# An encoder trunk whose first norm and first gate projection are interleaved two slices at a time

## The chip, the core and the metric

The kernel runs on one core of one Trainium2 chip. The metric is device time in microseconds (us); three runs of the kernel before gave 1000.81, 1001.91 and 1004.33, with a median of 1001.91.

## What is computed

Two layers on 256 tokens of 1024 values in float32. Each layer is a feed-forward block, a mixer (gated linear attention in the first layer, differential attention in the second) and another feed-forward block, each with an RMS norm ahead and a residual sum behind. Cut to the part that matters here, the first feed-forward block:

```python
def rms_norm(x, g):
    xf = x.astype(jnp.float32)
    y = xf * lax.rsqrt(jnp.mean(xf * xf, axis=-1, keepdims=True) + EPS)
    return (y * g.astype(jnp.float32)).astype(x.dtype)

def swiglu_ffn(h, w_gu, w_down):
    gate, up = jnp.split(h @ w_gu, 2, axis=-1)
    return (jax.nn.silu(gate) * up) @ w_down

x = x + 0.5 * swiglu_ffn(rms_norm(x, norm_g[i, 0]), ffn_w_gu[i, 0], ffn_w_down[i, 0])
```

The 1024 values of a token are eight slices of 128. The gate and the up projection have 2816 columns each, taken in groups of 256.

## The kernel before

Everything is kept transposed: the features on the 128 partitions, the tokens along the row. To get float32 accuracy from the faster float32r matmul, each operand is split into a high and a low part. ScalarE (ACT) writes the high part, rounded; VectorE (DVE) subtracts it from the whole and writes the low part. One slice of a projection is then a matmul over 512 columns with the high part of the weights (L181) and one over 256 columns with their low part (L182), in `mm3`.

**Weights.** `weight_plan` lists all weights as pieces of 1024 x 256 in order of use: weights 0 is the first gate group, weights 1 the first up group, weights 2 the second gate group, and so on. `prefetch` (L111) loads them on SyncE's queue (SP) into three staging buffers. A load waits until the low part of the weights three places earlier has been made, which frees its buffer. `next_weights` (L165) is called where a projection begins: it prefetches, has `split_weights` (L142) issue the splits of weights up to three ahead, and hands out the weights wanted.

**What sets the order.** The program is recorded in the order of the Python calls. A scheduler then puts each engine's instructions into one order; an engine runs its own strictly in that order. `tc.issue_after(i)` keeps an operation behind `i` on its engine. `split_weights` issues every split behind the operations in `state["behind"]`. `rsqrt` (L208), which computes the inverse root of the row statistics with twelve tiny DVE operations, ends so:

```python
            last = nc.vector.scalar_tensor_tensor(out=y, in0=t, scalar=1.5, in1=y, op0=ALU.add, op1=ALU.mult)
        state["behind"] += (last,)
```

so whatever is split by a later call stands behind it on DVE.

**The start.** `first_norm` (L397) loads x in three pieces on SP, then prefetches. The norm's weights (`rows`) come by GpSimd's queue (L230). TensorE (PE) runs eight idle matmuls, transposes `rows` (L406), whose copy `par` scales x, and then makes 16 transposes of 128 x 128 that turn x around (L413). Neighbouring slices of x lie in different PSUM banks, "so that two engines can follow each other". Per two slices, ACT and DVE split x twice (L276, L277) and then a quarter of weights 0 (L422). After the last quarter DVE copies x out of PSUM (L426), with the split of weights 1 (L432) between the copies, and the squares of x are taken and summed into `acc` (L285, L288, L289).

In `ffn` (L441) the first call of `next_weights` hands out weights 0 for the first gate group. Behind it come `norm.stats()` (two matmuls of `acc` into `ps_ms`, L294, then `rsqrt`), the join of the two halves of the gate (L205, L206), and the up projection:

```python
                pg = project(next_weights(), norm.x2, f"ps_g{c}", together=first and c == 0)
                if c == 0:
                    norm.stats()
                    if not first:
                        release(*state["behind"])
                gate = fp.tile([P, 2, T], F32, tag="gate", name="gate")
                join(pg, gate)
                pu = project(next_weights(), norm.x2, f"ps_u{c}")
                if c == 0:
                    norm.spread()
```

`norm.spread()` turns the result `r` around on PE (`ps_r`, L302).

Of the kernel before, what the change touches and what calls it, by code (L numbers as in the profile page):

```python
# [37 lines left out]
# the differential mixer: h half a projection; for pair of heads p: bp statistics, np normalized q and k,  # L38
# sph scores and softmax of head h, fp the transposed probabilities, ap their products with v, op normalized; hold keeps weights
# from being split  # L40
# [3 lines left out]
# the gated linear attention: h half a projection; z the gate's logits, y its log decay, pi prefix sums of pair of  # L44
# heads i, ri its scores before decay, d l t the next level's decays, scores and place among the scores,
# ai products with v, gi output gate, oi normalized; hold keeps weights from being split, x lets them go
# [8 lines left out]
def weight_plan(w):  # L55
    """The weights in the order of use: [rows, columns] pieces of at most 1024 x 256, slices of rows, columns, copies."""
# [17 lines left out]
    # four times side by side, to have the ranks on four groups of partitions  # L74
# [16 lines left out]
def trunk(ctx: ExitStack, tc: tile.TileContext, ins, out):  # L91
# [31 lines left out]
    def parts():  # L123
        """The parts of the next weights to split."""
# [26 lines left out]
    def issue(ops, after):  # L151
        """Each operation behind those of `after` that run on its engine."""
        with ExitStack() as order:
            for i in after:
                order.enter_context(tc.issue_after(i.ins))
            for op in ops:
                op()  # L157

    def release(*after):
        """The parts held back, behind `after`."""  # L160
        issue(held, after)
        held.clear()
        state["hold"] = None
# [8 lines left out]
    def mm1(ps, w, ms, act, k, first, last):  # L172
        """ps += wh.xh + wh.xl + wl.xh for one 128-deep slice."""
# [4 lines left out]
    def mm3(ps, w, ms, act, k, first, last, wk=None):  # L178
        """ps[:, 0:256] += wh.xh + wl.xh, ps[:, 256:512] += wh.xl for one 128-deep slice."""
# [4 lines left out]
    def project(w, act, name, together=False):  # L184
        banks = [psA.tile([P, 512], F32, tag="A", name=f"{name}_{b}") for b in range(2)]
        order = [(b, k) for b in range(2) for k in range(KD)]
        for b, k in sorted(order, key=lambda bk: bk[1]) if together else order:
            mm3(banks[b], w, slice(b * P, (b + 1) * P), act, k, k == 0, k == KD - 1)
        return banks
# [11 lines left out]
    def join(banks, out_t):  # L201
        """out = both halves of three-pass products."""
# [5 lines left out]
    def rsqrt(v, shape, name):  # L208
        """v ** -0.5 for v > 0."""
# [20 lines left out]
    nc.gpsimd.dma_start(rows, ins["norm_g"].rearrange("l s (k p) -> (l s k) p", p=P))  # L230
    nc.vector.memset(warm, 0.0)
    # the tensor engine runs at half its clock until it has been busy for a while
# [18 lines left out]
    def load_gate(w2):  # L251
        """The second gate weights as rows of high, low, high, low parts, zero against the other direction's ranks."""
# [54 lines left out]
    def down(act, nk, coef, norm):  # L307
        """x += coef * act @ w, and the next norm's blocks as they come."""
# [26 lines left out]
    def out_proj(act, norm, parts, late):  # L335
        """x += act @ w; the two first column groups wait for `late` with their last slices."""
# [28 lines left out]
    def by_token(xt):  # L365
        """x with the tokens on the partitions."""
# [10 lines left out]
    def down_out(act, nk, coef, xt):  # L377
        """out = x + coef * act @ w, with the tokens on the partitions."""
# [18 lines left out]
    def first_norm():  # L397
        n = Norm(0)
        with ExitStack() as xctx:
            xp = xctx.enter_context(tc.tile_pool(name="xin", bufs=1))  # L400
            x_tm = xp.tile([P, 2, D], F32, name="x_tm")
            for cs in (slice(0, CW), slice(CW, D // 2), slice(D // 2, D)):
                nc.sync.dma_start(x_tm[:, :, cs], ins["x"][0].rearrange("(t p) c -> p t c", p=P)[:, :, cs])
            prefetch(0)
# [3 lines left out]
            # neighbouring blocks lie in different banks, so that two engines can follow each other  # L408
            tiles = [psA.tile([P, 2, T], F32, tag="A", name=f"ps_x{i}") for i in range(KD // 2)]
            xt = [tiles[k // 4 * 2 + k % 2][:, k // 2 % 2, :] for k in range(KD)]  # L410
            for k in range(KD):
                for t in range(2):
                    nc.tensor.transpose(out=xt[k][:, t * P : (t + 1) * P], in_=x_tm[:, t, k * P : (k + 1) * P], identity=ident)  # L413
            last = ()
            for kp, ops in enumerate(parts()):
# [5 lines left out]
                with tc.issue_after(last[0].ins), tc.issue_after(last[1].ins):  # L421
                    last = [op() for op in ops]  # L422

            def keep(kp):
                k = kp // 2 * 4 + kp % 2
                return nc.vector.tensor_copy(x[:, k : k + 3 : 2, :], tiles[kp])  # L426
# [12 lines left out]
        return n  # L439

    def ffn(norm, nxt, first=False, beside=None):  # L441
        with ExitStack() as fctx:
            fp = fctx.enter_context(tc.tile_pool(name="ffn", bufs=2))
            a2 = fp.tile([P, NFB, 2, T], FR, tag="a2", name="a2", bufs=1)
            for c in range(FF // CW):
                if first and c == 3:
                    load_params()
                    relative_bias()
# [4 lines left out]
                pg = project(next_weights(), norm.x2, f"ps_g{c}", together=first and c == 0)  # L453
# [28 lines left out]
    def gla(norm, nxt, w2):  # L482
        QK = KD // 2
        with ExitStack() as gctx:
# [7 lines left out]
            with tc.tile_pool(name="glb", bufs=2) as lp:  # L492
                # gate path: low rank -> log decay -> prefix sums per tile of 128 tokens
# [6 lines left out]
                # both directions' ranks, twice the high parts, twice the low ones  # L500
# [8 lines left out]
                def project_half(kind, c, n):  # L509
                    """Half a column group: of q and k half the columns, of v and g half the tokens."""  # L510
# [459 lines left out]
```

## Time and profile before

| | us |
|---|---|
| median of three runs | 1001.91 |
| fastest and slowest run | 1000.81, 1004.33 |
| span of the profiled execution, first to last instruction | 1000.1 |
| PE busy in it | 994.5 |
| DVE busy | 748.0 |
| ACT busy | 567.7 |
| GpSimd (POOL) busy | 2.0 |

The profiled execution's own device time is not listed beside its span; the fastest run is 0.7 us above the span and the median 1.8 us. Times in the rows are microseconds from the start of the span, means of one instruction are in ns. PE is the matmul, PEld the load of the stationary operand, which overlaps it; a lower-case q behind an engine is its queue, where it issues transfers and waits. A PE duration is the time until its result is out, so two neighbours overlap; the step from one start to the next, or the chain's pieces, tell what a matmul costs.

### The profile page before, as it was taken

To read this page: it belongs to the slowest core of one execution; us is meant where nothing else is said; L and a number is where in the kernel's file an instruction comes from. 1 tells how busy PE (TensorE), PEld (TensorE's weight loads), DVE (VectorE), ACT (ScalarE), POOL (GpSimd) and SP (SyncE) were. 2 spreads that over 40 slices of the span, in tenths; PEclk is the share of its full clock that TensorE was granted. 3 is DMA by queue.
4 is the path that set the end of the run, shared out by engine and by line. 5 is a ranking of instruction groups with operands and counts; after the bars stand their busy time and mean duration, and the time that the engine had idled before them with its cause. 6 is when DMAs were issued, how large, how long until landed. Compare 5 with 4: busy or idle time off the path is not lost.

```text
span 1000.1 us, 16172 instructions
## 1 busy us (share of the span) xinstructions
PE 994.5 (99%) x6524; PEld 906.6 (91%) x6524; DVE 748.0 (75%) x1284; ACT 567.7 (57%) x962; POOL 2.0 (0%) x10
## 2 busy tenths in 40 slices
PE   9999999999999999999999999999999999999998
PEld 8888888999999888888888888889999998888998
DVE  6998756499877987774679787656989699767640
ACT  7666535397756755643456555435576577555430
POOL 0000000000000000000000000000000000000000
PEclk9999999999999999999999999999999999999999
DMA  9676544574322775545557555375655268555440
GB/s 295 221 263 209 190 158 135 194 226 154 127 85 85 256 248 178 190 159 187 167 176 248 195 184 178 128 240 171 194 149 169 65 200 274 178 171 193 158 132 22
DMA packets 176968, 178.95 MB, mean 179 GB/s; under 512 B 4419, under 2 KB 176222, under 8 KB 176894
## 3 DMA queue, kind: packets, MB, share of 16 engines
q1 hardware_dynamic: 176606, 177.68, 54.3%
q8 instruction: 51, 0.84, 0.3%
q10 hardware_dynamic: 256, 0.21, 0.1%
q14 instruction: 23, 0.19, 0.1%
q0 software_dynamic: 32, 0.02, 0.0%
HBM read 176.84 MB, written 1.06 MB: 178 GB/s over the span
## 4 chain that ended last, share of the span: by engine, by line
PE 98%; DVE 1%; DMA 0%; ACT 0%; issue 0%; ACTq 0%; POOLq 0%
PE ps_g L181 16%; PE ps_u L181 16%; PE ps_d L181 12%; PE ps_g L182 8%; PE ps_u L182 8%; PE ps_d L182 6%; PE ps_d L388 2%; PE ps_d L389 2%; PE ps_d L390 2%; PE ps_s L567 2%; PE ps_dqk L196 2%; PE ps_dqk L198 2%; PE ps_dqk L197 2%; PE ps_w L174 1%; PE ps_w L176 1%; PE ps_w L175 1%
## 5 line engine op out<-in xcount | busy, mean ns | idle before, releaser
L157 DVE TENSOR_TENSOR w<-stage,w 128x1024 fp32r<-128x1024 f32 x334 | 385.4, 1191 | 32.2 <-ACT w L157 31.9
L157 ACT ACTIVATE w<-stage 128x1024 fp32r<-128x1024 f32 x334 | 327.3, 1030 | 45.4 <-PE ps_d L390 17.0
L181 PE MATMUL ps_g<-x,w 128*128 128x512 f32 x704 | 249.3, 397 | 0.0
L181 PE MATMUL ps_u<-x,w 128*128 128x512 f32 x704 | 248.7, 395 | 0.0
L182 PE MATMUL ps_u<-x,w 128*128 128x256 f32 x704 | 197.5, 281 | 0.0
L182 PE MATMUL ps_g<-x,w 128*128 128x256 f32 x704 | 197.1, 281 | 0.0
L181 PE MATMUL ps_d<-a,w 128*128 128x512 f32 x528 | 183.2, 390 | 0.0
L181 PEld LDWEIGHTS ps_g<-x,w 128*128 128x128 f32 x704 | 132.0, 188 | 31.0 <-issue 0.9
L181 PEld LDWEIGHTS ps_u<-x,w 128*128 128x128 f32 x704 | 132.0, 188 | 30.7
L182 PE MATMUL ps_d<-a,w 128*128 128x256 f32 x528 | 149.0, 282 | 0.0
L182 PEld LDWEIGHTS ps_g<-x,w 128*128 128x128 f32 x704 | 133.4, 189 | 0.5
L182 PEld LDWEIGHTS ps_u<-x,w 128*128 128x128 f32 x704 | 133.1, 189 | 0.1
L181 PEld LDWEIGHTS ps_d<-a,w 128*128 128x128 f32 x528 | 99.1, 188 | 20.7
L182 PEld LDWEIGHTS ps_d<-a,w 128*128 128x128 f32 x528 | 99.9, 189 | 0.0
L276 ACT ACTIVATE x<-x,par 128x256 fp32r<-128x256 f32 x40 | 20.0, 507 | 117.5 <-DVE x L325 117.5
L205 ACT COPY half<-ps_u 128x256 f32<-128x256 f32 x88 | 32.7, 371 | 87.2 <-PE ps_u L182 85.4
L205 ACT COPY half<-ps_g 128x256 f32<-128x256 f32 x88 | 32.3, 370 | 83.5 <-PE ps_g L182 81.4
L206 DVE TENSOR_TENSOR up<-ps_u,half 128x256 f32<-128x256 f32 x88 | 36.9, 422 | 38.7 <-ACT half L205 38.6
L206 DVE TENSOR_TENSOR gate<-ps_g,half 128x256 f32<-128x256 f32 x88 | 36.8, 422 | 36.9 <-ACT half L205 36.9
L325 DVE SCALAR_TENSOR_TENSOR x<-ps_d,x 128x256 f32<-128x256 f32 x48 | 20.3, 424 | 57.9 <-PE ps_d L182 56.7
L388 PE MATMUL ps_d<-w,a 128*128 128x256 f32 x176 | 49.5, 281 | 0.0
L389 PE MATMUL ps_d<-w,a 128*128 128x256 f32 x176 | 49.5, 281 | 0.0
(232 smaller groups left out, 1560.6 us busy)
## 6 DMA issues: line engine op xcount, KB each, us to landing
stage<-in_ffn_w_gu_dram SPq DMA_DIRECT2D x86, 1024.0 KB, 5.1
stage<-in_ffn_w_down_dram SPq DMA_DIRECT2D x32, 1024.0 KB, 4.8
stage<-in_ffn_w_down_dram SPq DMA_DIRECT2D x16, 768.0 KB, 4.1
stage<-in_gla_w_in_dram SPq DMA_DIRECT2D x12, 1024.0 KB, 5.6
stage<-in_diff_w_in_dram SPq DMA_DIRECT2D x12, 1024.0 KB, 5.5
stage<-in_gla_w_out_dram SPq DMA_DIRECT2D x4, 1024.0 KB
stage<-in_diff_w_out_dram SPq DMA_DIRECT2D x4, 1024.0 KB, 4.9
stage<-in_ffn_w_gu_dram SPq DMA_DIRECT2D x8, 256.0 KB, 5.7
```

What stands on the lines that cost most here:

```text
L157: op()
L181: mm(ps, lhsT=w[:, wk, 0, ms], rhs=act[:, k, :, :], start=first, stop=False)
L182: mm(ps[:, 0:T], lhsT=w[:, wk, 1, ms], rhs=act[:, k, 0, :], start=False, stop=last)
L196: mm(ps[:, t, :], lhsT=act[:, k, 0, ts_], rhs=w[:, k, 0, :], start=k == 0, stop=False)
L197: mm(ps[:, t, :], lhsT=act[:, k, 0, ts_], rhs=w[:, k, 1, :], start=False, stop=False)
L198: mm(ps[:, t, :], lhsT=act[:, k, 1, ts_], rhs=w[:, k, 0, :], start=False, stop=k == KD - 1)
L205: nc.scalar.copy(h[:, b, :], ps[:, T:512])
L206: nc.vector.tensor_tensor(out=out_t[:, b, :], in0=ps[:, 0:T], in1=h[:, b, :], op=ALU.add)
L325: nc.vector.scalar_tensor_tensor(out=x[:, d, :], in0=ps[:, h * T : (h + 1) * T], scalar=coef, in1=x[:, d, :], op0=ALU.mult, op1=ALU.add,)
L388: mm(ps, lhsT=act[:, k0 + k, 0, ts_], rhs=w[:, k, 0, :], start=first, stop=False)
L389: mm(ps, lhsT=act[:, k0 + k, 0, ts_], rhs=w[:, k, 1, :], start=False, stop=False)
L390: mm(ps, lhsT=act[:, k0 + k, 1, ts_], rhs=w[:, k, 0, :], start=False, stop=last)
```

## The change

x is loaded in four pieces instead of three. The four quarters of weights 0 are loaded between them, two on ACT's queue and two on SP. The norm's weights come by ACT's queue instead of GpSimd's. The table and one-hot matrix of the relative-position bias, which had been loaded on ACT's queue at the start, move behind later work. `first_norm` becomes `first_group`: it brings two slices at a time (transposes, splits of x, split of the quarter) and puts the first gate group's matmuls of two slices behind the next two slices' transposes. Two neighbouring slices now share a PSUM bank. The first gate group no longer goes through `project` and `next_weights`, so in `ffn` the first call of `next_weights` is that of the first up group.

```diff
-    nc.gpsimd.dma_start(rows, ins["norm_g"].rearrange("l s (k p) -> (l s k) p", p=P))
+    nc.scalar.dma_start(rows, ins["norm_g"].rearrange("l s (k p) -> (l s k) p", p=P))
...
-    def first_norm():
+    def first_group():
...
-            for cs in (slice(0, CW), slice(CW, D // 2), slice(D // 2, D)):
+            src, nk, width, _ = plan[0]
+            t0 = staged[0] = stage.tile([P, KD, CW], F32, tag="stage", name="stage0")
+            state["dma"] = 1
+            for kp in range(KD // 2):
+                cs, ks = slice(kp * CW, (kp + 1) * CW), slice(2 * kp, 2 * kp + 2)
                 nc.sync.dma_start(x_tm[:, :, cs], ins["x"][0].rearrange("(t p) c -> p t c", p=P)[:, :, cs])
+                q = nc.scalar if kp < 2 else nc.sync
+                q.dma_start(t0[:, ks, :], src.rearrange("(k p) n -> p k n", p=P)[:, ks])
             prefetch(0)
...
-            # neighbouring blocks lie in different banks, so that two engines can follow each other
             tiles = [psA.tile([P, 2, T], F32, tag="A", name=f"ps_x{i}") for i in range(KD // 2)]
-            xt = [tiles[k // 4 * 2 + k % 2][:, k // 2 % 2, :] for k in range(KD)]
-            for k in range(KD):
-                for t in range(2):
-                    nc.tensor.transpose(out=xt[k][:, t * P : (t + 1) * P], in_=x_tm[:, t, k * P : (k + 1) * P], identity=ident)
+            xt = [tiles[k // 2][:, k % 2, :] for k in range(KD)]
+            split_parts = list(parts())
+            banks = [psA.tile([P, 512], F32, tag="A", name=f"ps_g0_{b}") for b in range(2)]
+            w0 = split.pop(0)
+            state["use"] = 1
             last = ()
-            for kp, ops in enumerate(parts()):
+
+            def bring(kp):
+                nonlocal last
+                for k in (2 * kp, 2 * kp + 1):
+                    for t in range(2):
+                        nc.tensor.transpose(out=xt[k][:, t * P : (t + 1) * P], in_=x_tm[:, t, k * P : (k + 1) * P], identity=ident)
                 for k in (2 * kp, 2 * kp + 1):
                     with ExitStack() as order:
                         for i in last:
                             order.enter_context(tc.issue_after(i.ins))
                         last = n.split(k, xt[k])
                 with tc.issue_after(last[0].ins), tc.issue_after(last[1].ins):
-                    last = [op() for op in ops]
+                    last = [op() for op in split_parts[kp]]
+
+            bring(0)
+            for kp in range(KD // 2):
+                if kp + 1 < KD // 2:
+                    bring(kp + 1)
+                for k in (2 * kp, 2 * kp + 1):
+                    for b in range(2):
+                        mm3(banks[b], w0, slice(b * P, (b + 1) * P), n.x2, k, k == 0, k == KD - 1)
...
                 if first and c == 3:
                     load_params()
-                    relative_bias()
+                    with tc.issue_after(state["behind"][0].ins):
+                        relative_bias()
...
-                pg = project(next_weights(), norm.x2, f"ps_g{c}", together=first and c == 0)
+                pg = first if first and c == 0 else project(next_weights(), norm.x2, f"ps_g{c}")
```

How the change moves instructions shows at three places. First PE, between the first up group and the second gate group. Before, PE goes on with the second gate group (`ps_g_0_354`, `ps_g_1_355`, weights `w_220`), and the statistics `ps_ms` stand behind the first matmul of the second up group (`ps_u_0_401`, weights `w_225`), 33 rows on:

```order
L182 MATMUL ps_u_1_296<-x_0_101,w_178 128x256
L181 MATMUL ps_g_0_354<-x_0_101,w_220 128x512
L182 MATMUL ps_g_0_354<-x_0_101,w_220 128x256
L181 MATMUL ps_g_0_354<-x_0_101,w_220 128x512
...
L182 MATMUL ps_g_1_355<-x_0_101,w_220 128x256
L181 MATMUL ps_u_0_401<-x_0_101,w_225 128x512
L294 MATMUL ps_ms_264<-cst,acc_102 128x1 x2
L182 MATMUL ps_u_0_401<-x_0_101,w_225 128x256
```

In the change, at the same place (the second gate group is now `ps_g_0_355` and `ps_g_1_356` with `w_281`, the second up group `ps_u_0_402` and `ps_u_1_403` with `w_286`, the third gate group `ps_g_0_456` and `ps_g_1_457` with `w_291`):

```order
L182 MATMUL ps_u_1_297<-x_0_101,w_213 128x256
L181 MATMUL ps_g_0_355<-x_0_101,w_281 128x512
L181 MATMUL ps_g_1_356<-x_0_101,w_281 128x512
L181 MATMUL ps_u_0_402<-x_0_101,w_286 128x512
L181 MATMUL ps_u_1_403<-x_0_101,w_286 128x512
L294 MATMUL ps_ms_255<-cst,acc_102 128x1 x2
L181 MATMUL ps_g_0_456<-x_0_101,w_291 128x512
L181 MATMUL ps_g_1_457<-x_0_101,w_291 128x512
L302 MATMUL ps_r_330<-cst,r_y 128x128 x2
L182 MATMUL ps_g_0_355<-x_0_101,w_281 128x256
L181 MATMUL ps_g_0_355<-x_0_101,w_281 128x512
```

The statistics, `ps_r` and the first matmuls of three groups now stand ahead of the second gate group's first L182, which reads the low part of weights 2.

Second DVE, from the sum of squares on. Before, the low parts of weights 2 and 3 (`w_220`, `w_225`) stand among the sums of squares, ahead of the statistics (`var`):

```order
L289 TENSOR_TENSOR acc_102<-acc_102,sq 128x256
L157 TENSOR_TENSOR w_220<-stage_120,w_220 128x4x256
L289 TENSOR_TENSOR acc_102<-acc_102,sq 128x256
L157 TENSOR_TENSOR w_220<-stage_120,w_220 128x4x256
L289 TENSOR_TENSOR acc_102<-acc_102,sq 128x256
L157 TENSOR_TENSOR w_225<-stage_122,w_225 128x4x256
...
L206 TENSOR_TENSOR up<-ps_u_0_295,half 128x256
L296 TENSOR_SCALAR var_267<-ps_ms_264 128x2
```

In the change (`w_281`, `w_286`, `w_291` are weights 2, 3 and 4):

```order
L206 TENSOR_TENSOR up<-ps_u_1_297,half 128x256
L289 TENSOR_TENSOR acc_102<-acc_102,sq 128x256
L296 TENSOR_SCALAR var_258<-ps_ms_255 128x2
L212 TENSOR_SCALAR r_t<-var_258 128x2
...
L216 TENSOR_TENSOR r_t<-r_t,var_258 128x2
L217 SCALAR_TENSOR_TENSOR r_y<-r_t,r_y 128x2
L157 TENSOR_TENSOR w_281<-stage_121,w_281 128x4x256 x2
L157 TENSOR_TENSOR w_286<-stage_123,w_286 128x4x256 x2
L157 TENSOR_TENSOR w_291<-stage_125,w_291 128x4x256 x2
```

All six pieces now stand behind the last operation of `rsqrt`.

Third ACT, over the same stretch. Before, four squares and two copies stand around the splits of weights 2 and 3:

```order
L288 ACTIVATE sq<-x 128x256 x2
L205 COPY half<-ps_g_1_231 128x256
L157 ACTIVATE w_220<-stage_120 128x4x256 x2
L205 COPY half<-ps_u_0_295 128x256
L288 ACTIVATE sq<-x 128x256
L157 ACTIVATE w_225<-stage_122 128x4x256 x2
L288 ACTIVATE sq<-x 128x256
```

In the change:

```order
L157 ACTIVATE w_281<-stage_121 128x4x256 x2
L205 COPY half<-ps_u_0_296 128x256
L157 ACTIVATE w_286<-stage_123 128x4x256
L288 ACTIVATE sq<-x 128x256 x2
L157 ACTIVATE w_286<-stage_123 128x4x256
L288 ACTIVATE sq<-x 128x256 x2
L205 COPY half<-ps_u_1_297 128x256
L288 ACTIVATE sq<-x 128x256
L157 ACTIVATE w_291<-stage_125 128x4x256 x2
```

Five of the eight squares now stand behind the first piece of weights 3, and the last of them behind the copy of the first up group's second half.

## Rows read from the trace of the kernel before

**Rows 1.** The page: busy time of the engines, and the last chain's shares.

```profile
PE 994.5 (99%) x6524; PEld 906.6 (91%) x6524; DVE 748.0 (75%) x1284; ACT 567.7 (57%) x962; POOL 2.0 (0%) x10
...
PE 98%; DVE 1%; DMA 0%; ACT 0%; issue 0%; ACTq 0%; POOLq 0%
```

**Rows 2.** PE's waits over the whole span: us in total, times, longest.

```profile
PE ps_idle L235 <- DVE warm L231: 0.9, 1, 0.9
PE ps_doT L891 <- DVE do L883: 0.7, 1, 0.7
PE ps_rows L406 <- DMA rows<-in_norm_g_dram: 0.7, 1, 0.7
```

**Rows 3.** The chain that ended last, from 4 to 16 us: start, us, what.

```profile
1.23 4.10 DMA rows<-in_norm_g_dram
...
5.37 0.34 PE ps_rows L406
5.71 3.60 PE ps_x L413 x16
9.31 0.85 PE ps_g L181 x2
10.16 0.36 PE ps_g L182 x2
10.52 0.23 PE ps_g L181
10.75 0.12 PE ps_g L182
```

**Rows 4.** DMA issues of the first 60 us: queue, count, KB each, median us to landing.

```profile
stage<-in_ffn_w_gu_dram SPq DMA_DIRECT2D x12, 1024.0 KB, 5.3
...
rows<-in_norm_g_dram POOLq DMA_DIRECT2D x1, 24.0 KB, 4.1
tab<-in_rel_bias_table_dram ACTq DMA_DIRECT2D x1, 1.0 KB, 3.9
```

**Rows 5.** ACT by time, 5 to 9 us, and its first issue of `tab`.

```profile
1.21 0.50 ACTq L725 DMA_DIRECT2D tab<-in_rel_bias_table_dram  x1
...
7.28 0.84 ACT L276 ACTIVATE x<-ps_x,par 128x256 fp32r<-128x256 f32 x2 [1.33 <-PE ps_x L413]
8.02 0.62 ACT L422 ACTIVATE w<-stage 128x512 fp32r<-128x512 f32 x1
```

**Rows 6.** DVE by time, 5 to 16 us.

```profile
7.78 0.88 DVE L277 SCALAR_TENSOR_TENSOR x<-ps_x,par,x 128x256 fp32r<-128x256 f32 x2 [6.92 <-ACT x L276]
8.67 0.69 DVE L422 TENSOR_TENSOR w<-stage,w 128x512 fp32r<-128x512 f32 x1
9.28 0.87 DVE L277 SCALAR_TENSOR_TENSOR x<-ps_x,par,x 128x256 fp32r<-128x256 f32 x2
...
12.83 0.69 DVE L422 TENSOR_TENSOR w<-stage,w 128x512 fp32r<-128x512 f32 x1
```

**Rows 7.** SP's queue by time: the issue that waits for `oh`, then the load of weights 3.

```profile
6.37 0.37 SPq L119 DMA_DIRECT2D stage<-in_ffn_w_gu_dram  x1
...
13.54 0.37 SPq L119 DMA_DIRECT2D stage<-in_ffn_w_gu_dram  x1
```

**Rows 8.** ACT by time, 14 to 20 us.

```profile
13.50 1.14 ACT L432 ACTIVATE w<-stage 128x512 fp32r<-128x512 f32 x2
...
15.39 0.73 ACT L288 ACTIVATE sq<-x 128x256 f32<-128x256 f32 x2
16.02 0.36 ACT L205 COPY half<-ps_g 128x256 f32<-128x256 f32 x1
16.27 2.01 ACT L157 ACTIVATE w<-stage 128x1024 fp32r<-128x1024 f32 x2
```

**Rows 9.** DVE by time, 24 to 50 us.

```profile
25.44 0.43 DVE L289 TENSOR_TENSOR acc<-acc,sq 128x256 f32<-128x256 f32 x1
...
27.34 0.16 DVE L296 TENSOR_SCALAR var<-ps_ms 128x2 f32<-128x2 f32 x1 [1.14 <-PE ps_ms L294]
...
28.55 0.15 DVE L215 SCALAR_TENSOR_TENSOR r_t<-r_y 128x2 f32<-128x2 f32 x1
...
30.10 0.16 DVE L217 SCALAR_TENSOR_TENSOR r_y<-r_t,r_y 128x2 f32<-128x2 f32 x1
30.18 2.35 DVE L157 TENSOR_TENSOR w<-stage,w 128x1024 fp32r<-128x1024 f32 x2
```

**Rows 10.** PE by time, 20.5 to 31.5 us.

```profile
20.91 0.40 PE L181 MATMUL ps_g<-x,w 128*128 128x512 f32 x1
21.15 0.28 PE L182 MATMUL ps_g<-x,w 128*128 128x256 f32 x1
...
26.80 0.50 PE L294 MATMUL ps_ms<-cst,acc 128*128 128x1 f32 x4
27.16 0.36 PE L182 MATMUL ps_u<-x,w 128*128 128x256 f32 x1
...
30.42 0.61 PE L302 MATMUL ps_r<-cst,r_y 128*128 128x128 f32 x4
30.79 0.36 PE L182 MATMUL ps_u<-x,w 128*128 128x256 f32 x1
```

More of the change, by code (lines that the diff above doesn't have):

```diff
@@ L182, in mm3, with project @@
         mm(ps[:, 0:T], lhsT=w[:, wk, 1, ms], rhs=act[:, k, 0, :], start=False, stop=last)
-    def project(w, act, name, together=False):
+    def project(w, act, name):
         banks = [psA.tile([P, 512], F32, tag="A", name=f"{name}_{b}") for b in range(2)]
-        order = [(b, k) for b in range(2) for k in range(KD)]
-        for b, k in sorted(order, key=lambda bk: bk[1]) if together else order:
-            mm3(banks[b], w, slice(b * P, (b + 1) * P), act, k, k == 0, k == KD - 1)
+        for b in range(2):
+            for k in range(KD):
+                mm3(banks[b], w, slice(b * P, (b + 1) * P), act, k, k == 0, k == KD - 1)
         return banks
@@ L421, in first_norm @@
                 with tc.issue_after(last[0].ins), tc.issue_after(last[1].ins):
-                    last = [op() for op in ops]
+                    last = [op() for op in split_parts[kp]]
[4 more added lines that the diff above has]
+                for k in (2 * kp, 2 * kp + 1):
+                    for b in range(2):
+                        mm3(banks[b], w0, slice(b * P, (b + 1) * P), n.x2, k, k == 0, k == KD - 1)
             def keep(kp):
-                k = kp // 2 * 4 + kp % 2
-                return nc.vector.tensor_copy(x[:, k : k + 3 : 2, :], tiles[kp])
+                return nc.vector.tensor_copy(x[:, 2 * kp : 2 * kp + 2, :], tiles[kp])
             with tc.issue_after(last[1].ins):
@@ L438, in first_norm, with ffn @@
                     n.square(k)
-        return n
-    def ffn(norm, nxt, first=False, beside=None):
+        return n, banks
+    def ffn(norm, nxt, first=None, beside=None):
         with ExitStack() as fctx:
@@ L916, in diff @@
         return n2
-    norm = first_norm()
+    norm, gate0 = first_group()
     with tc.tile_pool(name="gatew", bufs=1) as gw:
         w2 = gw.tile([P, 2, GH * DK], FR, name="w2")
-        norm = ffn(norm, 1, first=True, beside=lambda: load_gate(w2))
+        norm = ffn(norm, 1, first=gate0, beside=lambda: load_gate(w2))
         norm = gla(norm, 2, w2)
```

## The prediction

> **What bounds the kernel now.** I read the page's busy times and the shares of the last chain first: PE is busy for 994.5 of 1000.1 us and makes 98% of the chain [rows 1]. PE's list of waits comes next: three in the whole span, 0.9, 0.7 and 0.7 us, two of them ahead of 5.4 us [rows 2]. So nothing hides a delay of PE: whatever the change adds to or takes from PE's waits, the end moves by as much. The chain from 4 to 16 us says how the program starts: the norm's weights land at 1.23 + 4.10 = 5.33, PE turns them around at 5.37, then sixteen transposes run (3.60 us, 0.225 each), then the first gate group without a gap [rows 3]. The first two L181 take 0.85 us there, later ones 0.23 each: PE stood at the lower of its two clock levels (1.2 GHz) until about 10.2 and at the upper (2.4 GHz) after, though it had worked without a gap from 5.37 on.
>
> The number of PE's matmuls does not change, and from the third gate group on each engine's order is the old one but for neighbours changing places on ACT, DVE and SP. So I follow the program to the point where the orders meet again, and ask when PE gets there.
>
> **The change, step by step.**
>
> *1. The norm's weights by ACT's queue.* They become the second transfer there, in the place of `tab`, issued at 1.21 and landed 3.9 us later, at 5.1 [rows 4, 5]. The gain is bounded by PE's wait for them, 0.7 us [rows 2]; the loss by the third transfer of that queue, whose landing released SP's issue at 6.37 [rows 7], 1.0 later than 5.33. I take `tab`, its nearest row: 0.2 us gained. The smaller pieces of x and weights 0 I cost at nothing: the splits below need each later than it is loaded.
>
> *2. The first split.* ACT's first split of x waited for six transposes, since two more go into the same bank; now for four. It starts 0.2 + 2 x 0.225 earlier: 7.28 - 0.65 = 6.6 [rows 5], DVE's 0.5 later (7.28 to 7.78 [rows 5, 6]), at 7.1.
>
> *3. Slices that share a bank.* Before, ACT split one slice while DVE split its neighbour from another bank. Now both lie in one bank, and in the order ACT's second split waits for DVE's first. A round of two slices, from DVE's first split on: that split 0.47 (0.88/2 and a hand-over), ACT from its second split to the quarter of the weights 0.37 ((8.02 - 7.28)/2), to DVE's low part 0.65 (8.02 to 8.67), to DVE's next split 0.61 (8.67 to 9.28): 2.1 us [rows 5, 6]. Before, a round took (12.83 - 8.67)/3 = 1.39 [rows 6]. The first low part starts at 7.1 + 0.47 + 0.37 + 0.65 = 8.6, as before: step 1 and 2 are used up. The fourth is done at 8.6 + 3 x 2.1 + 0.69 = 15.6, where before it was 13.52: 2.1 us late. The Trainium skill, "PSUM — Partial Sum Buffer", section "PSUM bank collisions raise a hardware error", speaks against this layout: two engines may not touch one bank at the same time, reads included, so software has to make them take turns. If reads could overlap, the 1.39 of a round would stay and the sum below would be about 2 us smaller.
>
> *4. PE in this stretch.* The last transpose of the third pair of slices stands behind all matmuls of the first pair. At the lower clock these are four L181 (0.425 each), four L182 (half of that) and four transposes: 3.4 us from 8.6, so ACT's third round could begin at 12.3 instead of 10.8, 1.5 late; at the upper clock not late at all. PE now rests between the eighth transpose (about 7.2) and 8.6, and before, the clock was low for 4.8 us of unbroken work. That is nearest to the late end: I take 1.2. Weights 0 are split at 16.8, against 13.52.
>
> *5. Weights 3.* Their load waits for the buffer that this frees: issued at 13.54 before [rows 7], now at 16.9, landed 5.3 later [rows 4], at 22.2. ACT gets there at the same time: from its last quarter (16.1) four quarters of weights 1 (4 x 0.57), three squares (1.1), two copies (0.7), weights 2 (2.0), a copy (0.3): 22.5 [rows 8].
>
> *6. The statistics.* This is the term that decides. The first call of `next_weights` used to split weights 2 and 3 ahead of `norm.stats()`. Now the first call comes after it, and `rsqrt` has put its last operation into `state["behind"]`: the low parts of weights 2, 3 and 4 all stand behind `rsqrt` on DVE, and PE's second gate group, in whose way the statistics and `ps_r` stand too, needs the first of them. The chain: ACT from 22.5 half of weights 3 (1.0), two squares (0.73), the other half (1.0), two squares (0.73), the copy of the up group (0.36), the last square (0.4): 26.7 [rows 8]. DVE's last sum 0.43, to 27.1 [rows 9]. PE's statistics until DVE has them 0.54 (26.80 to 27.34 [rows 9, 10]), 27.65. Twelve tiny operations, nine of which took 28.55 to 30.26, so 0.19 each: 2.3, 29.95. Half the low part of weights 2 1.2 (2.35/2): 31.1 [rows 9]. Then PE's L182 of the second gate group starts. Before, it started at 21.15 [rows 10]. PE has done more by then: four L181 (0.93), the statistics (0.36) and `ps_r` (0.37) [rows 3, 10], 1.7 us that come later in the program before. So it is 31.1 - 22.8 = 8.3 us late.
>
> *7. PE's clock in the wait.* PE finishes the first up group at about 24 (the fourth quarter at 16.8, two copies 1.2, a low part 0.7, 30 matmuls 5.2) and the four hoisted L181 at 24.9. From there to 31.1 it has only 1.2 us of work. No row shows PE resting after it has reached the upper level. The ends are 0, if the level stays, and 2.4, half of the 4.8 us for which PE ran low after 5.37 [rows 3]; they lie equally far from what is known, and I take 1.2. The Trainium skill, "TensorE: Matmul & The Clock Gate", Part 1, says that idleness gates the clock to half and lasting work releases it. If this thin stretch counts as idle, that rule's sum is 1.2 us above mine; if not, 1.2 below.
>
> *8. After it.* DVE splits weights 2 to 4 until about 37.5. Weights 5, loaded when weights 2 are split (32.3 + 5.3), are wanted when PE is through three groups, after 46. Nothing else waits. The bias table's loads move behind ACT's splits, where no one waits for them before the middle of the block; I cost them at nothing, as long as PE's three groups (17 us) cover them.
>
> **Sum.** -0.2 and -0.45 at the start are inside the chain. 8.3 + 1.2 = 9.5 us. Against the profiled execution: 1000.1 + 9.5 = 1009.6 of span; the median stood 1.8 us above the span, so **1011.4**.
>
> **The rivals.**
>
> *The forecast: the wait forms.* Its low end: step 4 costs nothing and ACT is early, so only the end of the up group (15.6 + 1.2 + 0.7 + 5.2 = 22.7) holds the chain: copy, square, sum, statistics, `rsqrt`, low part (0.3 + 0.4 + 0.43 + 0.54 + 2.3 + 1.2) give 27.9, 5.1 us late, with no loss of clock: 1007.0. Its high end: the norm's weights land 1.0 late, 1.5 in step 4, 2.4 in step 7: 12.0 late, 1013.9. For it speaks that it is in the order, and each engine keeps its order. Chance 0.86.
>
> *Only the start is slower.* The splits of step 3 cost their 2.1 us, but the chain of step 6 hides behind work of PE that I have not seen. PE would then be 2 to 4 us late: 1004 to 1006. Against it: between the up group and the L182 stand only six L181. Chance 0.06.
>
> *Faster.* PE's wait for the norm's weights is the last one ahead of the first matmul, and now PE multiplies while x is still coming. If ACT and DVE read one bank without taking turns (a round of 1.39) and the low part of weights 2 were done before the up group ends, the start would be won: 0.2 to 0.7 us, and 0.45 from the fewer transposes, 1000.8 to 1001.3; with the transposes hidden in the matmuls' waits up to 3 us, 998.5. The point where it decides: `rsqrt` done before PE's up group ends. Its twelve operations (2.3 us) can't begin before the copy of that group's second half, which stands ahead of the last square on ACT. Chance 0.03.
>
> *The change does not do what it says.* Rows land no earlier, and the interleaving is lost in the order, so that everything takes its old time: 1001 to 1003. Chance 0.05.
>
> **How the numbers follow.** A measurement of this kernel tells 0.3%, 3 us, from no change. The forecast's whole range, 1007.0 to 1013.9, lies beyond; the second case straddles 1004.9, and I give it to slower by three quarters. Slower: 0.86 + 0.04 = 0.90; same: 0.05 + 0.02 + 0.01 of the faster case = 0.08; faster by over 0.3%: 0.02. The range of 1007 to 1014 leaves out the other cases (0.14).
>
> **What would show it.** The first split of x on ACT near 6.6; rounds of 2.1 us on DVE and a last low part of weights 0 near 16 to 17; weights 3 loaded then; in PE's list of waits a new one of some 6 us in pieces, ahead of `ps_ms`, `ps_r` and the L182 of the second gate group, with the last square, `rsqrt` and the low part of weights 2 in the chain; that L182 near 31. L181 of 0.43 instead of 0.23 behind it would show the lower clock. I am wrong if PE's waits after 10 us sum to under 3 us, if DVE's rounds stay at 1.4, or if the second gate group goes on before 27.

## The result, and the profile after

The changed kernel takes 1013.06 us (median of 4 runs, 1012.76 to 1014.56), the kernel before in the same job 1002.15 (1000.81 to 1004.33): a ratio of 1.0112, with a 95% interval of 1.0098 to 1.0126. The forecast was 1011.4, in a range of 1007 to 1014. The span of the profiled execution is 1012.7 us against 1000.1.

The page's busy times, to be read beside [rows 1]:

```profile
PE 1000.8 (99%) x6524; PEld 908.3 (90%) x6524; DVE 750.2 (74%) x1284; ACT 567.7 (56%) x962; POOL 1.4 (0%) x9
```

PE runs the same 6524 instructions, and its busy time is 6.3 us longer; the span is 12.6 longer. So about half of the loss is rest and half is matmuls that took longer. PE's list of waits (us in total, times, longest) had three entries before [rows 2]. Now:

```profile
PE ps_ms L294 <- DVE acc L289: 1.7, 1, 1.7
PE ps_rows L413 <- DMA rows<-in_norm_g_dram: 1.4, 1, 1.4
PE ps_g L181 <- DVE x L277: 1.3, 1, 1.3
...
PE ps_r L302 <- DVE r_y L217: 0.9, 1, 0.9
PE ps_g L181 <- ACT w L157: 0.7, 1, 0.7
...
PE ps_g L181 <- ACT w L434: 0.5, 2, 0.3
```

`ps_ms`, `ps_r` and one L181 are the pieces of the wait that the prediction described: 3.3 us in all, and between them PE had two statistics matmuls, two L181 and `ps_r` to do. The old entries, `ps_idle` and `ps_doT`, are left out here. `ps_rows` and the two other entries of L181 belong to the start. The chain that ended last, from 1 to 33 us (start, us, what), answers to [rows 3]:

```profile
1.22 4.70 DMA rows<-in_norm_g_dram
...
6.05 0.31 PE ps_rows L413
...
7.50 0.48 ACT x L276
8.01 0.50 DVE x L277
...
17.38 0.70 DVE w L434
18.10 5.19 DMA stage<-in_ffn_w_gu_dram
...
25.94 0.61 ACT sq L288 x2
...
27.48 0.42 DVE acc L289
27.95 0.62 PE ps_ms L294 x4
28.59 0.17 DVE var L296
...
30.77 0.17 DVE r_y L217
30.98 1.23 PE ps_r L302 x4
32.21 0.49 PE ps_g L182
32.70 0.43 PE ps_g L181
```

Read it from the bottom: the second gate group's L182 waits for `ps_r` and the low part behind the inverse root, that for the statistics, they for the last sum of squares, ACT's squares for the split of weights 3, the split for the load, and the load for the buffer that the last low part of weights 0 frees at 18.1. Before, that buffer was free at 13.52 [rows 6, 7]. The steps of DVE show where the start became late (start, us, engine, line, operation; in brackets the idle time before it and what ended it):

```profile
8.01 0.48 DVE L277 SCALAR_TENSOR_TENSOR x<-ps_x,par,x 128x256 fp32r<-128x256 f32 x1 [7.15 <-ACT x L276]
...
10.17 0.48 DVE L277 SCALAR_TENSOR_TENSOR x<-ps_x,par,x 128x256 fp32r<-128x256 f32 x1
...
13.69 0.48 DVE L277 SCALAR_TENSOR_TENSOR x<-ps_x,par,x 128x256 fp32r<-128x256 f32 x1 [1.30 <-ACT x L276]
...
15.84 0.48 DVE L277 SCALAR_TENSOR_TENSOR x<-ps_x,par,x 128x256 fp32r<-128x256 f32 x1
...
30.84 5.76 DVE L157 TENSOR_TENSOR w<-stage,w 128x1024 fp32r<-128x1024 f32 x5
```

A round of two slices takes 2.15 us (8.01 to 10.17, 13.69 to 15.84) where it took 1.39 [rows 6], and the third begins 1.37 us later still. The last line is the block of low parts behind the inverse root; [rows 9] had two pieces there, because the earlier ones had gone ahead of the statistics. ACT by time gives the reasons for both:

```profile
8.53 0.47 ACT L276 ACTIVATE x<-ps_x,par 128x256 fp32r<-128x256 f32 x1 [0.55 <-DVE x L277]
...
13.18 0.47 ACT L276 ACTIVATE x<-ps_x,par 128x256 fp32r<-128x256 f32 x1 [1.51 <-PE ps_x L427]
...
23.32 1.06 ACT L157 ACTIVATE w<-stage 128x1024 fp32r<-128x1024 f32 x1 [0.16 <-DMA stage<-in_ffn_w_gu_dram]
```

ACT's second split of a pair waits 0.55 for DVE's split from the same bank, and the third pair for its transposes, which stand behind the first pair's matmuls. Last the stretches around the wait (from and to, length, busy time and instructions of PE, PEld, DVE, ACT, POOL, granted clock, DMA share, GB/s):

```profile
24.00:28.00 4.00, 2.27 (x13) 1.62 (x11) 2.82 (x8) 3.15 (x8) 0.00 (x0) 1.00 0.58 198
28.00:32.00 4.00, 2.36 (x10) 1.70 (x10) 3.02 (x14) 2.00 (x2) 0.00 (x0) 0.73 0.06 19
32.00:36.00 4.00, 4.00 (x13) 3.40 (x13) 4.00 (x5) 0.37 (x1) 0.00 (x0) 0.50 0.37 110
36.00:40.00 4.00, 4.00 (x23) 3.48 (x23) 2.67 (x4) 0.75 (x3) 0.00 (x0) 0.92 1.09 361
```

PE was busy for 2.27 and 2.36 of 4 us in two stretches, and from 32 to 36 the granted clock is 0.50, the lower level (1.2 GHz): 13 matmuls in 4 us, where the following stretch has 23. The fall shows in the second of the two stretches already (0.73), while PE still waits: `ps_r` took 1.23 us at 30.98, where it was 0.61 before [rows 10]. PE by time, first in the kernel before, then in the changed one:

```profile
45.36 0.49 PE L181 MATMUL ps_g<-x,w 128*128 128x512 f32 x1
```

```profile
36.72 0.40 PE L182 MATMUL ps_g<-x,w 128*128 128x256 f32 x2
...
56.59 0.50 PE L181 MATMUL ps_g<-x,w 128*128 128x512 f32 x1
```

The account against the profile before: the second gate group's first L182 starts at 32.12. In the program before it stood at 21.15, with one L181 ahead of it where six stand now; with five L181 (1.16), the statistics (0.36) and `ps_r` (0.37) added, its old place is 23.0, so it is 9.1 late. The third gate group goes on behind the bias's matmul at 56.59 instead of 45.36, 11.2 late, and the 2.1 between are the clock's: from that L182 seven steps to the next L182 take 4.60 us (32.12 to 36.72), where before they took 2.47 (21.15 to 23.62). At the first down projection PE is 12.9 late (147.15 against 134.21), without a wait in between, and the span ends 12.6 late; the last section comes back to that.

### The profile page after: what moved, and what is told of

It reads as the page before. It is cut to its first block, busy times and chain, and to the rows that moved or that the text cites. A ratio compares the mean times of both kernels' runs of the same rounds, so it can differ in the third digit from the quotient of the medians.

```text
span 1012.7 us, 16166 instructions
## 1 busy us (share of the span) xinstructions
PE 1000.8 (99%) x6524; PEld 908.3 (90%) x6524; DVE 750.2 (74%) x1284; ACT 567.7 (56%) x962; POOL 1.4 (0%) x9
## 4 chain that ended last, share of the span: by engine, by line
PE 96%; DVE 2%; DMA 1%; ACT 1%; issue 0%; ACTq 0%
PE ps_g L181 16%; PE ps_u L181 16%; PE ps_d L181 12%; PE ps_g L182 8%; PE ps_u L182 8%; PE ps_d L182 6%; PE ps_d L390 2%; PE ps_d L388 2%; PE ps_d L389 2%; PE ps_s L587 2%; PE ps_dqk L196 2%; PE ps_dqk L198 2%; PE ps_dqk L197 2%; PE ps_w L174 1%; PE ps_w L175 1%; PE ps_w L176 1%
## 5 line engine op out<-in xcount | busy, mean ns | idle before, releaser
L181 PE MATMUL ps_g<-x,w 128*128 128x512 f32 x704 | 252.7, 401 | 2.5 <-DVE x L277 1.3
L181 PE MATMUL ps_u<-x,w 128*128 128x512 f32 x704 | 249.2, 396 | 0.0
L182 PE MATMUL ps_g<-x,w 128*128 128x256 f32 x704 | 198.5, 283 | 0.0
L182 PE MATMUL ps_u<-x,w 128*128 128x256 f32 x704 | 197.2, 281 | 0.0
L181 PE MATMUL ps_d<-a,w 128*128 128x512 f32 x528 | 183.2, 390 | 0.0
L181 PEld LDWEIGHTS ps_g<-x,w 128*128 128x128 f32 x704 | 133.1, 190 | 35.1 <-ACT w L434 2.8
L181 PEld LDWEIGHTS ps_u<-x,w 128*128 128x128 f32 x704 | 132.1, 188 | 31.3 <-PE ps_g L182 0.2
L182 PE MATMUL ps_d<-a,w 128*128 128x256 f32 x528 | 148.9, 282 | 0.0
L182 PEld LDWEIGHTS ps_g<-x,w 128*128 128x128 f32 x704 | 134.3, 191 | 1.3 <-DVE w L434 0.9
L182 PEld LDWEIGHTS ps_u<-x,w 128*128 128x128 f32 x704 | 133.0, 189 | 0.5 <-DVE w L451 0.3
L181 PEld LDWEIGHTS ps_d<-a,w 128*128 128x128 f32 x528 | 99.1, 188 | 20.8
L182 PEld LDWEIGHTS ps_d<-a,w 128*128 128x128 f32 x528 | 99.8, 189 | 0.0
L206 DVE TENSOR_TENSOR up<-ps_u,half 128x256 f32<-128x256 f32 x88 | 36.9, 421 | 40.5 <-ACT half L205 40.4
L206 DVE TENSOR_TENSOR gate<-ps_g,half 128x256 f32<-128x256 f32 x88 | 36.8, 420 | 40.2 <-ACT half L205 39.9
```

The source lines that it names most:

```text
L181: mm(ps, lhsT=w[:, wk, 0, ms], rhs=act[:, k, :, :], start=first, stop=False)
L182: mm(ps[:, 0:T], lhsT=w[:, wk, 1, ms], rhs=act[:, k, 0, :], start=False, stop=last)
L206: nc.vector.tensor_tensor(out=out_t[:, b, :], in0=ps[:, 0:T], in1=h[:, b, :], op=ALU.add)
```

## Experiments

Ratios are against the kernel before in the same job, with their 95% intervals; 0.001 is 1.0 us. Expectations speak of medians of the job in which they were written.

**1. The early split put back.** `split_weights(0)` is called at the end of `first_group`, as the first `next_weights` used to do, ahead of the statistics; all else stays.

```diff
+        split_weights(0)
         return n, banks
```

> The changed kernel, with weights 2 and 3 split ahead of the statistics again, as before the change. Theory (the low parts of weights 2 to 4 stand behind rsqrt, and PE's second gate group behind them): the wait of PE ahead of ps_ms, ps_r and the second gate group goes, and with it the lower clock behind it; what stays is the late start. In the changed kernel the first up group's L182 began at 19.93 where it was 15.74 before, so 4.2 us over the kernel before remain, about 1006 us, PE's waits after 20 us are under 1 us, and the second gate group's L182 starts near 25.4. Rival (the late start alone makes the wait, since weights 0 are split 4.5 us late and weights 3 are loaded late): the wait stays for the most part, 1010 us or more.

1006.84 us, 1.0031 (1.0019 to 1.0043). PE's waits for the statistics are gone; beside the old entries of `ps_idle` and `ps_doT` the list holds only one, at the start:

```profile
PE ps_g L181 <- ACT w L434: 2.9, 3, 2.4
```

and DVE makes the low parts of weights 2 and 3 among the sums again, from 22.04 on, ahead of `var` at 30.38. So one call moved gives back 8 of 11 us. The other 3 are in the start: the first up group starts at 18.10, where it was 15.28 before. The second gate group's L182 came at 24.30, 1.1 ahead of the expectation.

**2. The old banks.** Neighbouring slices of x in different PSUM banks again.

```diff
-            xt = [tiles[k // 2][:, k % 2, :] for k in range(KD)]
+            xt = [tiles[k // 4 * 2 + k % 2][:, k // 2 % 2, :] for k in range(KD)]
...
```

> The changed kernel, with neighbouring slices of x in different PSUM banks, as before the change; the splits of weights 2 to 4 stay behind rsqrt. Theory: ACT and DVE follow each other again, rounds of 1.4 us instead of 2.1, but the third round still waits for PE at the lower clock until about 13.2; weights 0 are split by 16.6 instead of 18.1, and the whole is 1.5 us faster than the changed kernel, about 1011.5 us. The long wait of PE ahead of ps_ms and ps_r stays. Rival (the shared banks are the cause): 4 us or more faster than the changed kernel, under 1009 us.

1011.31 us, 1.0073 (1.0055 to 1.0090). The wait stays:

```profile
PE ps_g L181 <- DVE up L206: 1.8, 1, 1.8
PE ps_ms L294 <- DVE acc L289: 1.3, 1, 1.3
PE ps_g L181 <- ACT w L434: 1.1, 1, 1.1
```

Weights 0 are split 1.8 us earlier (the last low part at 15.54 instead of 17.38), and the L182 behind the wait starts at 30.04 instead of 32.12; of these 2.1 us, 1.0 is the norm's weights, which were turned at 5.01 here and at 6.05 in the changed kernel's profile. By the ratios the gain over the change is 3.9 us, nearer the rival's 4 than the expected 1.5, by the two spans 2.1 (1010.6 against 1012.7), so its size stays open. What the list shows is that the banks are not what makes the wait.

**3. Both.** The diffs of experiments 1 and 2 in one kernel.

> Both at once: old banks, and weights 2 and 3 split ahead of the statistics. Theory: what is left is the start alone, the late norm's weights (0.6 us) and PE's lower clock in the third round: 2.7 us over the kernel before, about 1005 us, no wait of PE after 20 us. Rival (interleaving two slices costs nothing by itself once banks and order are as before, and starts earlier): the time before or under, 1001 to 1002 us.

1006.68 us, 1.0023 (1.0007 to 1.0040), in a job where the kernel before took 1004.03: slower than before by what the theory said, and not back at the old time. No wait for the statistics is left in the profile. The start lost something of its own; experiment 8 returns to it.

**4. The late split alone, in the kernel before.** The first gate group takes weights 0 without calling `next_weights`; start, queues and banks stay old.

```diff
-                pg = project(next_weights(), norm.x2, f"ps_g{c}", together=first and c == 0)
+                if first and c == 0:
+                    state["use"] = 1
+                    pg = project(split.pop(0), norm.x2, f"ps_g{c}", together=True)
+                else:
+                    pg = project(next_weights(), norm.x2, f"ps_g{c}")
```

> The kernel before, changed in one thing: the first gate group takes weights 0 without calling next_weights, so that weights 2 and 3 are split behind rsqrt. Start, banks and queues are those of before. Theory: the wait forms by itself: the copy of the up group, two pieces of weights 3 and four squares on ACT, the last sum, the statistics, rsqrt and the low part put the second gate group's first L182 near 27.6 instead of 21.15, 4.9 us of delay net of what PE has done by then, and 2.3 us more if the clock falls as in the changed kernel: 1006.8 to 1009.3 us. Rival (the wait comes from the late start): under 1003 us.

1011.81 us, 1.0077 (1.0060 to 1.0095). The wait forms with the old start too; PE's list and DVE's block behind the inverse root:

```profile
PE ps_x L413 <- DMA x_tm<-in_x_dram: 2.0, 1, 2.0
PE ps_r L302 <- DVE r_y L217: 1.8, 1, 1.8
```

```profile
28.24 6.90 DVE L157 TENSOR_TENSOR w<-stage,w 128x1024 fp32r<-128x1024 f32 x6
```

By the ratio it is 7.7 us slower, a little more than expected; in the profiled execution PE waited 2.0 us for x, of which the expectation knew nothing. The first up group starts 2.3 us later there than before (17.56 against 15.28), and the L182 behind the wait stands at 29.51 instead of 27.6.

**5. The tie alone.** The call stays late; only the last operation of the first inverse root is no longer added to `state["behind"]`.

```diff
-        state["behind"] += (last,)
+        if name != "r0":
+            state["behind"] += (last,)
```

> The changed kernel, the first norm's inverse root no longer added to the operations that every later split stands behind; the call that splits weights 2 to 4 stays where the change put it. Theory (the tie makes the wait): the low parts of weights 2 and 3 may stand ahead of the statistics again, the second gate group goes on at 25.5 to 27 us without a list of waits behind the up group, and the time is that of the kernel with the early split, 1005 to 1008. Rival (it is the late call itself, or the late squares on ScalarE): the wait stays, 1010 or more.

1003.76 us, 1.0023 (1.0009 to 1.0036): 8.9 us of the changed kernel's 11 are gone. The late call by itself costs nothing that can be measured: the scheduler, left free, puts the low parts where the early call had them. DVE and PE by time (the lines are numbered one higher here):

```profile
23.89 1.22 DVE L157 TENSOR_TENSOR w<-stage,w 128x1024 fp32r<-128x1024 f32 x1
...
30.90 0.15 DVE L297 TENSOR_SCALAR var<-ps_ms 128x2 f32<-128x2 f32 x1
```

```profile
25.16 0.39 PE L182 MATMUL ps_g<-x,w 128*128 128x256 f32 x1
```

The second gate group goes on at 25.16 without a wait. The inverse root itself is pulled apart by splits, and `ps_r` comes at 40.66 instead of 30.98; nothing waited for it.

**6. Control and filler: the clock's share.** The control records the first statistics behind the up projection and holds the low parts back until then, which leaves the wait; the second kernel adds idle matmuls in it, eight ahead of the statistics and eleven behind (the control has one each).

```diff
+                if c == 0 and first:
+                    last = fill(8, state["mm"])
+                    with tc.issue_after(last.ins):
+                        norm.stats()
+                    release(*state["behind"])
+                    fill(11, norm.ms)
...
```

> The control for the next run. The changed kernel with its first statistics recorded behind the up projection and the low parts still held behind the inverse root, and one idle matmul ahead of the statistics and one behind them. Both theories: the changed kernel's time, 1013 (1011.5 to 1014.5), the second gate group's first L182 at about 32 us, and L181 of 0.43 us behind it.

> The control with eight idle matmuls of TensorE ahead of the statistics and eleven behind them, so that it multiplies through the wait. Theory: the wait's rest cost 2.3 us of clock on top; with the wait filled, L181 behind it take 0.23 us at once, the group's first L182 stands at the same 32 us or up to 0.7 later, and the end comes 1.5 to 2.3 us before the control's, at about 1011. Rival: the clock falls for another reason, or the fillers only push the work back: L181 still 0.43 behind the wait, and the time within 0.7 us of the control or above it.

The control took 1010.91 us, 1.0087 (1.0065 to 1.0109); with the filler 1008.83, 1.0065 (1.0047 to 1.0082): 2.1 us less, though PE did 34 more matmuls (each idle one counts as two). The control lies 0.6 below the range expected for it, and the intervals overlap, so the times alone do not settle the clock's share; the profiles show it. Control, the stretch behind the wait (columns as above) and its first matmuls:

```profile
32.00:36.00 4.00, 4.00 (x16) 3.48 (x17) 4.00 (x4) 0.00 (x0) 0.00 (x0) 0.62 0.44 139
```

```profile
31.90 0.58 PE L182 MATMUL ps_g<-x,w 128*128 128x256 f32 x1 [0.36 <-DVE w L157]
32.28 0.63 PE L181 MATMUL ps_g<-x,w 128*128 128x512 f32 x1
32.71 0.41 PE L182 MATMUL ps_g<-x,w 128*128 128x256 f32 x1
...
35.17 0.27 PE L182 MATMUL ps_g<-x,w 128*128 128x256 f32 x1
```

Filled, the same two views:

```profile
32.00:36.00 4.00, 4.00 (x24) 3.49 (x24) 4.00 (x5) 0.37 (x1) 0.00 (x0) 1.00 0.60 194
```

```profile
31.25 0.39 PE L182 MATMUL ps_g<-x,w 128*128 128x256 f32 x1
31.47 0.39 PE L181 MATMUL ps_g<-x,w 128*128 128x512 f32 x1
31.70 0.28 PE L182 MATMUL ps_g<-x,w 128*128 128x256 f32 x1
...
33.11 0.28 PE L182 MATMUL ps_g<-x,w 128*128 128x256 f32 x1
```

From the L181 to the next L182 it is 0.43 us in the control and 0.23 filled, at once. Work that computes nothing kept the clock at the upper level (2.4 GHz). What that is worth is read from five steps, L182 to L182: 3.27 us in the control (31.90 to 35.17), 1.86 filled (31.25 to 33.11), so 1.4 us. The filled group's start, 0.65 earlier, is not the filler's: the norm's weights were turned 0.9 earlier in that profile (5.13 against 6.07), and the inverse root was done 0.65 earlier. So the 2.1 us between the medians is not the clock's price alone.

**7. A longer warm-up in the kernel before.** Ten idle matmuls at the start instead of eight.

```diff
-WARM = 8
+WARM = 10
```

> The kernel before with ten idle matmuls at the start instead of eight, so that TensorE works on until the norm's weights land. Theory: the short rest ahead of those weights keeps the clock at its lower level; without it the sixteen transposes take 0.13 us each instead of 0.225 and the first L181 0.23, and the first up group starts up to 1.2 us earlier: 1001.0 to 1001.7 against 1002.2. Rival: ScalarE's and VectorE's splits (1.39 us per two slices) bound the start whatever TensorE's clock: the first up group starts within 0.3 us of before, and the time is 1002.2 or, where the idle matmuls push the weights' transpose back, up to 1 us more.

1001.91 us, 1.0000 (0.9983 to 1.0017). The first eight transposes took 0.14 us each (1.10/8), as at the upper level, but then PE waited for x, and behind that rest the next eight took 0.21:

```profile
5.74 1.10 PE L413 MATMUL ps_x<-cst,x_tm 128*128 128x128 f32 x8
8.75 1.70 PE L413 MATMUL ps_x<-cst,x_tm 128*128 128x128 f32 x8 [1.92 <-DMA x_tm<-in_x_dram]
```

In the profile before, the ninth transpose follows the eighth without a wait, at about 7.5; here x came only at 8.7, as in experiment 4, where the warm-up was the old one. The profiled execution thus tests neither theory; the times say that nothing is won.

**8. Banks and tie undone, and the queue of the norm's weights.** The diffs of experiments 2 and 5 in one kernel, and the same with the norm's weights by GpSimd's queue:

```diff
-    nc.scalar.dma_start(rows, ins["norm_g"].rearrange("l s (k p) -> (l s k) p", p=P))
+    nc.gpsimd.dma_start(rows, ins["norm_g"].rearrange("l s (k p) -> (l s k) p", p=P))
```

> The changed kernel with two of its parts undone: neighbouring slices of x in different banks again, and the first inverse root not added to the operations that every later split stands behind. Theory (bank sharing and the tie were priced by themselves and add up): the run without the tie stood 0.2% above the kernel before and the banks gave 1.7 us beside the tie, so 1001 to 1003.5, within 0.2% of before. Rival (the pieces at the start cost something of their own, in landing times or in PE's transposes between matmuls): it stays 2 us or more above before, as the run with the early split and the old banks did, 1004 or more.

> The same with the norm's weights by GpSimd's queue again. Theory (the queue of the norm's weights makes no difference that the landing times' own scatter of about 1 us does not cover): within 1 us of the run with ScalarE's queue. Rival (by ScalarE's queue they land later, 5.9 against 5.3 us): 0.6 us or more faster than that run, with the norm's weights turned at 5.2 to 5.4 us.

The kernel before took 1003.32 in this job. By ScalarE's queue 1005.09 us, 1.0012 (1.0001 to 1.0024): by the ratio as the theory had it, by the time in the rival's 1004 or more, as the kernel before stood 1.3 above the 1001.99 that the figures were built on. The interval leaves the two undecided. By GpSimd's 1005.30, 1.0018 (1.0009 to 1.0027). In the two profiles the norm's weights were turned at 4.54 and at 6.48, 1.9 us apart and the other way round than [rows 3] and the changed kernel's chain had it, and the times are 0.2 apart. Neither is faster than the kernel before. PE does begin sooner (the first gate group at 6.97 in the first of the two against 8.96 before), but ends no sooner: the first up group starts at 15.74 against 15.28. Of the 2.0 us at its first matmul 0.8 are the norm's weights, which were turned earlier in that profile. Counted from that turn, the first up group starts after 11.2 us by ScalarE's queue and 10.9 by GpSimd's, and after 9.9 before. What is left is on ACT in that kernel:

```profile
10.43 0.90 ACT L277 ACTIVATE x<-ps_x,par 128x256 fp32r<-128x256 f32 x2 [1.57 <-PE ps_x L428]
...
12.55 0.84 ACT L277 ACTIVATE x<-ps_x,par 128x256 fp32r<-128x256 f32 x2 [0.70 <-PE ps_x L428]
```

ACT waits for the transposes of the third and fourth pair, which stand behind the matmuls of the first and second; those run at the lower clock after PE's rests for the splits (granted 0.57 from 7 to 10 us). DVE's low parts of weights 0 start at 6.95 and 13.95: 2.33 a round, where it was 1.39 [rows 6]; by GpSimd's queue it is 2.33 too (8.59 to 15.58). So the interleaved kernels have longer rounds with either choice of banks. How long a round would be with all of it at the upper clock was not run; the fourth pair, which is at that level, still waits 0.70. No kernel of these beats the one before.

## Why the prediction was right

Point by point, by its own steps:

*1, the norm's weights:* the sign was wrong. They landed at 5.92, 0.6 later than before, not 0.2 earlier, and the first split of x began at 7.50 instead of 6.6. No single row could tell: over the profiles they are turned at 4.5 to 6.1 us by ScalarE's queue and at 5.2 to 6.5 by GpSimd's.

*2 and 3, banks and rounds:* 2.1 us forecast, 2.15 measured, with ACT's wait for DVE as the cause. The Trainium skill's rule that software has to keep two engines from one PSUM bank at the same time ("PSUM — Partial Sum Buffer", section "PSUM bank collisions raise a hardware error") agrees with the 0.55 of that wait. Without bank sharing the round stays long for another reason (experiment 8), so in the end's time the banks cost only 1.1 us without the tie (1.0023 to 1.0012), 0.8 between experiments 1 and 3, and 3.9 between the change and experiment 2; the intervals let all three be about 1 to 2.

*4, PE at the lower clock delays the third round:* 1.2 taken, 1.37 measured. (3.4 us from 8.6 give 12.0 and not 12.3, so the late end was 1.2 by its own terms.) Weights 0 were split at 18.1 instead of 16.8; 0.9 of that is the late first split.

*5, weights 3:* issued at 18.10 and landed at 23.29, with ACT there 0.16 earlier: the coincidence of load and ACT was right, 1 us later than forecast.

*6, the statistics and the tie:* the term that decides was right in its mechanism. Undoing the tie alone gives back 8.9 us, undoing the banks alone does not remove the wait, and the late call alone makes it in the old kernel with its old start. Its size was 8.3 forecast and 9.1 measured. The 8.3 is itself a miscount: it takes four L181 as done ahead of the L182, but six stand there (the prediction's own second rival has them) and one did before, so five, and 31.1 would have been 8.1 late. The 1.0 that is missing came in with the start: weights 0 were 1.3 late, of which ACT's last square was only 0.45 late (27.15 against 26.7), and a join of the up group (L206) ahead of the last sum, which the account had left out, brought 0.35 more. "Some 6 us in pieces" was too much for the list of waits, which shows 3.3; the L182 stands where it does because what PE does between the pieces, it does in the meantime and slowly.

*7, the clock:* this term was mis-sized as well: "the ends are 0 ... and 2.4 ... I take 1.2". It took nearly the whole upper end, 2.1 in the account of the profile; between the control, whose low stretch was shorter, and the filled kernel it was 1.4. The middle between two ends was a poor choice: the granted clock did fall in the wait and stayed low behind it (0.50 in the changed kernel and 0.62 in the control from 32 to 36 us, 0.50 in experiment 4 from 28 to 32), and in the filled one it stayed at 1.00. The Trainium skill's rule that idleness gates the clock to half ("TensorE: Matmul & The Clock Gate", Part 1) agrees with that, and by it the forecast would have been 1012.6, against 1013.06 measured.

*8, nothing behind it:* no wait appeared later. The sum was 9.5 and the medians differ by 10.9. Steps 6 and 7 were each about 1 us too small, in the same direction; the range held because its high end had late weights, the late end of step 4 and 2.4 of step 7 in it, and that is nearly what came.

Of the rivals, "only the start is slower" is what remains when the tie is undone: 1.0023, at the low edge of its 1004 to 1006. "Faster" failed at the point named for it: the inverse root was done at 30.9, the up group's matmuls at 25.3. And where that point is removed (experiment 8), the start is still not won: the splits wait for transposes that now stand behind matmuls, a round is 2.33 long instead of 1.39, and what PE gains at its first matmul (2.0 us, 0.8 of them because the norm's weights came early in that profile) is gone by the last.

## What to carry to other kernels

When a call moves past another in the program, look for lists that the other one appends to: a line that ties later work "behind" some operation ties whatever is now recorded after it, and PE can end up waiting for work that needed nothing from that operation. Where such a wait leaves PE with little to do, cost the matmuls behind it at the lower clock and not at the middle of the two levels: here that was 2.1 us. Where the stretch can't be removed, idle matmuls in it kept the upper clock and bought back 1.4 us by the profiles. An earlier first matmul was worth nothing here, as it delayed the transposes that the next splits wait for.

## What was not expected of the hardware

**Landing times at the start scatter.** The same transfers land at different times from one profile to the next: the norm's weights let PE go on at 4.5 to 6.5 us, and x kept PE waiting for 2.0 and 1.9 us in two of the profiles (experiments 4 and 7) and not at all in others. A term of under 1 us at the start can't be read from one profile.

**Two paces of the same matmuls.** Later in the feed-forward blocks, with no wait and a granted clock of 1.00, a group of 32 matmuls took 5.55 us in the profile before (56.56 to 62.11) and 5.65 in the changed one (62.35 to 68.00). Over the 16 groups between, that is the 1.7 us from 11.2 late at the third gate group to 12.9 at the down projection. Both paces occur in the profiles of both kernels, so it is not charged to the change; what sets them stays open.

**A slow stretch without a sign in the clock column.** In the kernel before, L181 took 0.43 us at 9.31 to 10.16 [rows 3] while that stretch's granted clock is given as 1.00; in the early-split run the same matmuls show 0.50. At the start the durations tell the level, the column does not always.
